# Pacing and pinning the modulation and gate steps of a two-layer hybrid decoder trunk

## The chip, the cores and the metric

The kernel runs on one core of one Trainium2 chip. The metric is the time of one execution on the device, in microseconds; the median of the runs is compared. The profile shows one execution, with the core's engines: PE (TensorE, matrix multiply; PEld is its weight load), DVE (VectorE), ACT (ScalarE), POOL (GpSimd) and SP (SyncE, which here issues every DMA).

## The reference, cut to what matters

Two decoder layers over 512 tokens of width 1024, all in float32. Each layer does this:

```python
shift, scale, gate = split(silu(c) @ w_ada + b_ada, 3)
h = rms_norm(x, ln_pre) * (1 + scale) + shift
u = split_columns(h @ w_in)
o_a = dilated_attention(u['a_q'], u['a_k'], u['a_v'])
o_b = nsa_attention(u['b_q'], ...)
o_c = rms_norm(gla_attention(u['c_q'], u['c_k'], u['c_v'], log_a), gla_norm)
o_d = banded_attention(u['d_q'], u['d_k'], u['d_v'], SWA_WIN - 1, sinks)
mixed = concat([o_a * silu(u['a_z']), ..., o_d * silu(u['d_z'])])
x = x + gate * rms_norm(mixed @ w_out, ln_post)
```

What the change moves about is the first line: the product of the one row `silu(c)` with the 1024 x 3072 matrix `w_ada` of a layer. It depends on no other work of the layer. Two thirds of it, shift and scale ("modulation"), are needed when the next layer begins; the last third ("gate") when the layer ends.

## The kernel before, in words

Matrices are multiplied in two parts: every weight tile `wraw` that comes from memory is split into a rounded part `whi` (ScalarE, L478) and the rest `wlo` (VectorE, L481), every activation into HH and HL, and three matmuls make one product. For each chunk of 128 columns of `w_in`, `mm_T` (L528) issues 24 matmuls of 512 columns; `mm_TM` (L540) is the same with tokens and columns exchanged; `fin_T` and `fin_tm` empty the accumulators on ScalarE and VectorE (for the compressed keys by the copies `x`, L619 and L621). `proj` (L652) goes through all chunks, `out1` (L1226) does the output projection as far as groups C, B and A reach, and `out2` (L1248) the rest with the norm and the residual add.

The four attention groups run in the order C, B, A, D. `attn_c` (L822) is a chain of products over levels of a chunked linear attention (the tiles zp, dp, bp, kq, att, oc); the others consist of `unit` (L755): scores on PE, maximum and mask on VectorE (L766), exponential on ScalarE (L768), scaling on VectorE (L777, L779), transposes on PE (L782), copies back (L787, L789).

**The first line of the reference runs on VectorE.** `extras` (L362) is a generator that goes through units of work, one per turn. For layer 0 these are 32 modulation steps for layer 1 (`mod`, L288: one multiply-and-sum of a 128 x 512 tile `wmod` with the broadcast row, L293) and then 16 gate steps (`mac`, L349: the tile `wada` times one value per partition, added to `aac`, L351 and L353). For layer 1 there are the 16 gate steps alone. The gate comes in two halves of 8 steps; when a half is done, `fin` (L373) adds over the partitions with a matmul of a matrix of ones (`ada`, L380), adds the bias (`adab`, VectorE, L381) and multiplies by the norm's weights (`gl`, POOL, L383). Each step's tile, 256 KB, is loaded one step ahead, by SP, into a pool of two buffers (`ad`), which the two rows that `fin` loads (L377, L379) share. `out2` reads `gl` at L1284.

**What orders the work.** The program is traced in one order; a scheduler then sets each engine's order ahead of the run: among the instructions that its own model of the machine takes as ready, the one traced first goes first. `pin()` (L524) adds an edge that keeps the PE instructions of a block behind PE's projection matmul traced last, without a wait on its result. On the chip every engine works through its own order, and so does SP's queue, where a load waits until its buffer is free.

`merge` (L1310) makes the order of the trace. It goes through the stages (attention C, B, A and four parts of D), takes a step of attention, then as many steps of the projection `pg` as a ratio of estimated costs allows; the generators yield these costs (1.3 for six matmuls of `mm_T`; 24 (n + 8) / 2400 for one `mm_TM`). Every projection cost goes through `bg`, which counts it up and takes one turn of `extras` for each `pace` that is full:

```python
            def bg(cost):
                tick[0] += cost
                while tick[0] > pace:
                    tick[0] -= pace
                    next(BG[0], None)
```

`pace` comes from the list TK of the layer, by stage (C, B, A, all of D). Whatever of `extras` is left behind the stages is traced at L1378. The first turn of `extras` only loads; each later turn does one unit.

Of the kernel before, what the change touches and what calls it, by code (L numbers as in the profile page):

```python
# [7 lines left out]
F32 = mybir.dt.float32  # L8
F32R = mybir.dt.float32r
AF = mybir.ActivationFunctionType  # L10
ALU = mybir.AluOpType
# [31 lines left out]
STP = 0  # L43

LP = [
    dict(HC=30, HB=[60, 60, 60, 200, 200, 200, 200, 120], HA=60, HD=200, RC=0.9, RB=0.7, RA=1.4, RD=0.8, TK=[1.5, 1.5, 1.5, 1.5], PT=(4, 3),
         HO=(0, 2, 1, 3)),
    dict(HC=30, HB=[60, 60, 60, 60, 60, 60, 60, 200], HA=100, HD=30, RC=0.9, RB=0.8, RA=0.8, RD=1.4, TK=[1.0, 6.0, 1.2, 0.7], PT=(1, 0),
         HO=(0, 3, 1, 2)),
]  # L50
WLO_MOD, WLO_POOL = 5, ()
# [182 lines left out]
def build(tc, A, out_d):  # L234
    nc = tc.nc
    PE, ACT, DVE, POOL, SP = nc.tensor, nc.scalar, nc.vector, nc.gpsimd, nc.sync
    with ExitStack() as ctx:
        def pool(name, bufs, **kw):
            return ctx.enter_context(tc.tile_pool(name=name, bufs=bufs, **kw))
# [8 lines left out]
        ad_p = pool('ad', B['ad'])  # L248
# [9 lines left out]
        def ps_t(tag, name):  # L258
            return ps.tile([128, 512], F32, tag=tag, name=name)
# [4 lines left out]
        def s_t(name, n, bufs=None):  # L264
            return sm_p.tile([128, n], F32, tag=name, name=name, **({'bufs': bufs} if bufs else {}))
# [16 lines left out]
        def load_mod(l, n, p, tag):  # L282

            wt = p.tile([128, 512], F32, tag=tag, name='wmod')
            SP.dma_start(out=wt, in_=A['w_mod'][l, n // 4, n // 2 % 2, n % 2])
            return wt

        def mod(l, n, wt, ss, gs):  # L288

            o, c = _P['bada'][0], n // 2  # L290
            h = n % 2
            init, dst = (tmp[:, c:c + 1], ss[:, c:c + 1]) if h else (pars[l][:, o + c:o + c + 1], tmp[:, c:c + 1])
            DVE.tensor_tensor_reduce(wt, wt, csr[:, 512 * h:512 * h + 512], 0.5, init, ALU.mult, ALU.add, dst)  # L293
            if n % 4 == 3:
                j = n // 4
                o = _P['lnpre'][0]
                DVE.scalar_tensor_tensor(gs[:, j:j + 1], ss[:, c:c + 1], 1.0, pars[l][:, o + j:o + j + 1], op0=ALU.add, op1=ALU.mult)
# [3 lines left out]
        def load_par(l):  # L301
            t = pp.tile([128, P_TOT], F32, tag='par', name='par')
            SP.dma_start(out=t, in_=A['par'][l])
            pars.append(t)

        WR = {}
        for ch in FIRST:
# [8 lines left out]
            elif ch in 'TQ':  # L316
                n = 'tm_c' if ch == 'T' else 't_cqk'
                WR[n] = [raw_p.tile([128, 1024 if ch == 'Q' else 996], F32, tag='raw', name='wraw')]
                SP.dma_start(out=WR[n][0], in_=A['w_in'][0, W_OFF[n, 0]:W_OFF[n, 0] + 128 * WR[n][0].shape[1]].rearrange('(p n) -> p n', p=128))
            else:  # L320
                i = len(x_t)
# [7 lines left out]
        ones = cp.tile([128, 1], F32, name='ones')  # L329
# [19 lines left out]
        def mac(acc, w, k, first):  # L349
            if first:  # L350
                DVE.tensor_scalar(acc, w, csil[:, k:k + 1], None, op0=ALU.mult)  # L351
            else:
                DVE.scalar_tensor_tensor(acc, w, csil[:, k:k + 1], acc, op0=ALU.mult, op1=ALU.add)  # L353

        def halves(t):
# [3 lines left out]
            DVE.tensor_tensor(out=lo, in0=t, in1=hi, op=ALU.subtract)  # L359
            return hi, lo  # L360

        def extras(l):  # L362

            units = []
            if l + 1 < DEPTH:
                load_par(l + 1)
                ss, gs = s_t('adass', 16, 2), s_t('adags', 8, 2)
                ada[l + 1] = (gs, ss)
                units = [(2, n) for n in range(32)]
            units += [(n, k) for n in range(2) for k in range(8)]  # L370
            gl[l] = []

            def fin(n, sb):  # L373
                acc = ps_t('s', 'ada')
                o = 512 * n
                br = ad_p.tile([128, 512], F32, tag='ad', name='adab')
                SP.dma_start(out=br, in_=A['rows'][l, 0, :, o:o + 512].to_broadcast([128, 512]))  # L377
                lr = ad_p.tile([128, 512], F32, tag='ad', name='adal')
                SP.dma_start(out=lr, in_=A['rows'][l, 1, :, o:o + 512].to_broadcast([128, 512]))  # L379
                PE.matmul(acc, ones.to_broadcast([128, 128]), sb, start=True, stop=True)  # L380
                DVE.tensor_tensor(out=br, in0=acc, in1=br, op=ALU.add)  # L381
                g = sz_p.tile([128, 512], F32, tag='sz', name='gl')
                POOL.tensor_tensor(out=g, in0=br, in1=lr, op=ALU.mult)  # L383
                gl[l].append(g)

            def load(n, k):
                if n == 2:
                    return load_mod(l + 1, k, ad_p, 'ad')
                wt = ad_p.tile([128, 512], F32, tag='ad', name='wada')
                SP.dma_start(out=wt, in_=A['w_gate'][l, n, k])  # L390
                return wt
            nxt = load(*units[0])
            prev = None
            for u, (n, k) in enumerate(units):
                yield
                wt = nxt
                if prev:
                    fin(*prev)
                    prev = None
                if n == 2:  # L400
                    mod(l + 1, k, wt, ss, gs)
                else:
                    if k == 0:
                        sb = ad_p.tile([128, 512], F32, tag='aac', name='aac', bufs=1)
                    mac(sb, wt, k, k == 0)
                    if k == 7:
                        prev = (n, sb)
                if u + 1 < len(units):
                    nxt = load(*units[u + 1])
            yield  # L410
            fin(*prev)

        gl, ada = {}, {}
# [61 lines left out]
        def split_w(raw, n, eng=None):  # L475
            hi = w_p.tile([128, n], F32R, tag='whi', name='whi')
            lo = w_p.tile([128, n], F32R, tag='wlo', name='wlo')
            ACT.copy(hi, raw)  # L478
            nsplit[0] += 1
            eng = eng or (POOL if nsplit[0] % WLO_MOD in WLO_POOL else DVE)  # L480
            eng.tensor_tensor(out=lo, in0=raw, in1=hi, op=ALU.subtract)  # L481
            return hi, lo

        def load_piece(l, name, i, kk, ncol):
# [39 lines left out]
        def pin():  # L524

            return tc.issue_after(LASTP[0]) if LASTP[0] is not None else nullcontext()
# [125 lines left out]
        def proj(l, skip=0):  # L652
            for n_, (name, cols) in enumerate(CHUNKS[skip:]):
                n = len(cols)
                w = WS[l].get(len(_parts(name, cols)))
                WS[l].ahead(PRE)
                yield 0.0
                if name.startswith('tm'):
                    for i in range(4):
                        fin_tm(l, name, i, mm_TM(l, w, i, n))  # L660
                        yield 24 * (n + 8) / 2.4e3
                elif name == 't_cqk':
                    for j in range(2):
                        fin_T(l, ('cq', 'ck')[j], (yield from mm_T(l, w, 128 * j, 128)))
                        yield 1.3
                else:
                    fin_T(l, name, (yield from mm_T(l, w, 0, n)))
                    yield 1.3
# [634 lines left out]
        def run(g):  # L1303
            for _ in g:
                pass
# [4 lines left out]
        def merge(l, pg, steps):  # L1310

            acc = 0.0
            tick = [0.0]
            done = False
# [5 lines that stand above are left out]
                    next(BG[0], None)  # L1320
            for n_, (g, names, ratio, lead) in enumerate(steps):
                pace = LP[l]['TK'][min(n_, 3)]
                while not all(n in T for n in names):
                    bg(next(pg))
                lead = list(lead)
                while True:
                    n = lead.pop(0) if len(lead) > 1 else lead[0]
                    tc.cur_priority -= n
                    cost = next(g, None)
                    tc.cur_priority += n  # L1330
                    if cost is None:
                        break
                    acc += cost * ratio
                    while acc > 0 and not done:
                        d = next(pg, None)
                        if d is None:
                            done = True
                        elif d < 0:
                            break
                        else:  # L1340
                            acc -= d
                            bg(d)
            if not done:
                run(pg)

        x1 = dr.tile([512, 1024], F32, tag='x1', name='x1', bufs=1)
        WS[0] = Stream(0, 2)
# [2 lines left out]
        def chain(*gs):  # L1350
            for g in gs:
                yield from g
# [8 lines left out]
        for l in range(DEPTH):  # L1361
# [4 lines left out]
            pg = chain(proj(l, 1 if l else 2), out1(l))  # L1366
# [51 lines left out]
```

## Time and profile before

| what | value |
|---|---|
| median of 3 runs | 699.97 us (698.76 to 700.46) |
| the profiled execution's own time | 701.64 us |
| its span, first to last instruction | 699.9 us |
| mean granted clock of TensorE | 0.979 |
| busy: PE, PEld, DVE, ACT, POOL | 648.1, 525.2, 496.6, 332.1, 30.0 us |
| chain that ended last, by engine | PE 62%, DVE 16%, DMA 7%, ACT 6%, issue 5%, SPq 2% |

The span is that of the one execution that the profile shows; some 1.7 us of its time lie outside. Matmuls are pipelined and their ends are modelled, so PE is marked busy even where it is not at its peak. PEclk is the clock that the throttle granted, as a share of 2.4 GHz; 0.5 is 1.2 GHz. "Idle before" is the time in which an engine stood still before an instruction, with what ended it.

The stages can be told by their instructions: attention C of layer 0 runs from some 57 to 147 us, B to 245, A to 300, D to 342 (with the output projection), `out2` and the head of the next layer to 386; attention C of layer 1 to 480, B to 575, A to 640, the rest to the end.

### The profile page before, as it was taken

What the parts mean: (1) busy time and instruction counts of PE and PEld (TensorE: products, weight loads), DVE (VectorE), ACT (ScalarE), POOL (GpSimd) and SP (SyncE); (2) the same over time, 40 slices, a digit from 0 to 9 for tenths busy, and PEclk for the clock granted to TensorE, in tenths of its full rate; (3) what the DMA queues carried; (4) which work ended last, traced back from release to release, by engine and by line L of the source; (5) the groups of instructions that cost most, each with busy time, mean ns of one, the idle gap of its engine ahead of it and who ended that gap; (6) DMA issues with size and microseconds to landing.
All of it is one profiled execution on the core that took longest, in us unless ns stands there. A gap on an engine that the chain in (4) does not pass through costs nothing.

```text
span 699.9 us, 11964 instructions
## 1 busy us (share of the span) xinstructions
PE 648.1 (93%) x4460; PEld 525.2 (75%) x4460; DVE 496.6 (71%) x1291; ACT 332.1 (47%) x744; POOL 30.0 (4%) x57
## 2 busy tenths in 40 slices
PE   3997888899999999999998978999999999999996
PEld 1775776787677777679986756888777877778895
DVE  5994878675978765785598458464398778757756
ACT  5454443172556554573476236246346346434532
POOL 2000001000000000000011000000000000000000
PEclk9999899899999999999999989999999999999999
DMA  8957755566342412002642772212620021011233
GB/s 296 391 224 199 225 183 168 159 200 236 101 131 79 162 45 75 33 16 76 210 164 84 233 191 75 62 62 66 206 61 23 10 90 46 31 45 46 76 124 118
DMA packets 38163, 87.89 MB, mean 126 GB/s; under 512 B 4185, under 2 KB 7769, under 8 KB 38106
## 3 DMA queue, kind: packets, MB, share of 16 engines
q1 hardware_dynamic: 38106, 87.14, 38.9%
q8 instruction: 35, 0.57, 0.3%
q14 instruction: 22, 0.18, 0.1%
HBM read 81.88 MB, written 5.24 MB: 124 GB/s over the span
## 4 chain that ended last, share of the span: by engine, by line
PE 62%; DVE 16%; DMA 7%; ACT 6%; issue 5%; SPq 2%; POOL 1%; DVEq 0%; POOLq 0%; ACTq 0%
PE mmT L534 22%; PE yo L1221 9%; PE mmTM L547 7%; PE pT L782 5%; DVE wmod L293 3%; DMA wmod<-in_w_mod 3%; PE ob L796 3%; PE sc L649 2%; DMA wada<-in_w_gate 2%; DVE wlo L481 2%; PE yo L1268 2%; PE sc L650 2%; PE oa L796 2%; PE od L1055 2%; ACT whi L478 1%
## 5 line engine op out<-in xcount | busy, mean ns | idle before, releaser
L534 PE MATMUL mmT<-HH,whi 128*128 128x512 f32 (+1 forms) x352 | 146.4, 416 | 6.8 <-ACT x L619 6.8
L534 PE MATMUL mmT<-HL,whi 128*128 128x512 f32 (+1 forms) x352 | 142.3, 405 | 0.0
L534 PE MATMUL mmT<-HH,wlo 128*128 128x512 f32 (+1 forms) x352 | 141.9, 404 | 0.0
L768 ACT ACTIVATE p<-p,m 128x256 f32<-128x256 f32 (+3 forms) x128 | 68.8, 539 | 79.6 <-DVE m L766 76.8
L481 DVE TENSOR_TENSOR wlo<-wraw,whi 128x1024 fp32r<-128x1024 f32 (+3 forms) x60 | 72.1, 1202 | 28.1 <-ACT whi L478 27.8
L478 ACT CAST whi<-wraw 128x1024 fp32r<-128x1024 f32 (+3 forms) x60 | 61.4, 1026 | 53.5 <-PE mmT L534 29.9
L534 PEld LDWEIGHTS mmT<-HH,whi 128*128 128x128 f32 (+1 forms) x352 | 67.4, 191 | 25.0 <-ACT x L619 8.3
L534 PEld LDWEIGHTS mmT<-HH,wlo 128*128 128x128 f32 (+1 forms) x352 | 67.0, 190 | 15.2 <-issue 1.2
L534 PEld LDWEIGHTS mmT<-HL,whi 128*128 128x128 f32 (+1 forms) x352 | 67.2, 191 | 13.1 <-issue 1.0
L766 DVE CUSTOM_DVE_ANT_0 p<-sc,cst 128x128 f32<-128x128 f32 (+3 forms) x96 | 44.8, 481 | 16.1 <-PE sc L650 15.6
L782 PE MATMUL pT<-cst,p 128*128 128x128 f32 x296 | 49.1, 279 | 4.7 <-DVE p L779 1.9
L547 PE MATMUL mmTM<-whi,HH 128*128 128x256 f32 (+1 forms) x160 | 48.6, 304 | 2.9 <-ACT HH L470 2.4
L782 PEld LDWEIGHTS pT<-cst,p 128*128 128x128 f32 x296 | 33.5, 140 | 20.0 <-issue 8.8
L547 PE MATMUL mmTM<-whi,HL 128*128 128x256 f32 (+1 forms) x160 | 48.0, 300 | 0.4 <-DVE HL L471 0.4
L547 PE MATMUL mmTM<-wlo,HH 128*128 128x256 f32 (+1 forms) x160 | 47.6, 298 | 0.0
L1221 PE MATMUL yo<-whi,HL 128*128 128x256 f32 x144 | 41.5, 289 | 0.0
L1221 PE MATMUL yo<-whi,HH 128*128 128x256 f32 x144 | 41.5, 288 | 0.0
L1221 PE MATMUL yo<-wlo,HH 128*128 128x256 f32 x144 | 41.5, 288 | 0.0
L789 DVE COPY pt<-pT 128x256 f32<-128x256 f32 (+3 forms) x60 | 28.9, 500 | 10.6 <-PE pT L782 7.8
L547 PEld LDWEIGHTS mmTM<-whi,HH 128*128 128x128 f32 x160 | 31.3, 196 | 5.7 <-ACT HH L470 3.5
L293 DVE CUSTOM_DVE_ANT_0 wmod<-wmod,csr,par 128x512 f32<-128x512 f32 x32 | 23.6, 746 | 13.7 <-DMA wmod<-in_w_mod 13.7
L649 PE MATMUL sc<-k,x 128*128 128x128 f32 (+3 forms) x96 | 32.1, 344 | 1.0 <-DVE m L766 1.0
(274 smaller groups left out, 1340.2 us busy)
## 6 DMA issues: line engine op xcount, KB each, us to landing
wraw<-in_w_in SPq DMA_DIRECT2D x52, 512.0 KB
wmod<-in_w_mod SPq DMA_DIRECT2D x64, 256.0 KB
wada<-in_w_gate SPq DMA_DIRECT2D x32, 256.0 KB
wor<-in_w_out SPq DMA_DIRECT2D x12, 512.0 KB
w<-in_w SPq DMA_DIRECT2D x8, 512.0 KB
vs<-vd SPq DMA_DIRECT2D x24, 128.0 KB
x<-in_x SPq DMA_DIRECT2D x8, 256.0 KB
wor<-in_w_out SPq DMA_DIRECT2D x8, 256.0 KB
```

What stands on the lines that cost most here:

```text
L293: DVE.tensor_tensor_reduce(wt, wt, csr[:, 512 * h:512 * h + 512], 0.5, init, ALU.mult, ALU.add, dst)
L478: ACT.copy(hi, raw)
L481: eng.tensor_tensor(out=lo, in0=raw, in1=hi, op=ALU.subtract)
L534: LASTP[0] = PE.matmul(acc[:m], a, b, start=(n == 0), stop=(n == 23)).ins
L547: LASTP[0] = PE.matmul(acc[:, :ncol], a, b, start=(n == 0), stop=(n == 23)).ins
L649: PE.matmul(out, q[e][:, qs], k[e][0][:, ks], start=True, stop=False)
L766: DVE.tensor_tensor_reduce(p[:, c], sc[:, c], mask, -0.125, 1e38 if sink is None else sink[0][:, es[j]:es[j] + 1], ALU.add, ALU.min, m[:, ...
L768: ACT.activation(p[:, c], p[:, c], AF.Exp, bias=m[:, j:j + 1], scale=-1.0, accum_out=lsum[:, j:j + 1])
L782: PE.transpose(tp[:, b:b + 128], p[:, b:b + 128], C('ident'))
L789: DVE.tensor_copy(dst, src)
L796: PE.matmul(o[hs, q0:q1], vt[:, kb, vc:vc + 64], PT[:, 512 * kb:512 * kb + q1 - q0], start=(first and kb == 0), stop=(last and kb == 3), s ...
L1221: LASTP[0] = PE.matmul(acc[:, :n_], a, b, start=(n == 0), stop=(n == last)).ins
```

## The change

The paces become other numbers, with a fifth for the projection steps that are left when the stages are through; at the start of each stage the count is cut to the stage's pace. `fin`'s matmul is pinned behind PE's projection matmul traced last, and `fin` comes four turns later than before. The VectorE instructions of each modulation and gate step get an edge that keeps them behind VectorE's instruction traced last at that moment (the object LO only tells which engine that is). The loads are not pinned. All arithmetic stays the same.

```diff
@@ -43,9 +43,9 @@
 STP = 0
 
 LP = [
-    dict(HC=30, HB=[60, 60, 60, 200, 200, 200, 200, 120], HA=60, HD=200, RC=0.9, RB=0.7, RA=1.4, RD=0.8, TK=[1.5, 1.5, 1.5, 1.5], PT=(4, 3),
+    dict(HC=30, HB=[60, 60, 60, 200, 200, 200, 200, 120], HA=60, HD=200, RC=0.9, RB=0.7, RA=1.4, RD=0.8, TK=[3.0, 2.0, 1.8, 1.0, 1.2], PT=(4, 3),
          HO=(0, 2, 1, 3)),
-    dict(HC=30, HB=[60, 60, 60, 60, 60, 60, 60, 200], HA=100, HD=30, RC=0.9, RB=0.8, RA=0.8, RD=1.4, TK=[1.0, 6.0, 1.2, 0.7], PT=(1, 0),
+    dict(HC=30, HB=[60, 60, 60, 60, 60, 60, 60, 200], HA=100, HD=30, RC=0.9, RB=0.8, RA=0.8, RD=1.4, TK=[99.0, 2.5, 2.0, 2.0, 2.0], PT=(1, 0),
          HO=(0, 3, 1, 2)),
 ]
 WLO_MOD, WLO_POOL = 5, ()
@@ -359,6 +359,11 @@
             DVE.tensor_tensor(out=lo, in0=t, in1=hi, op=ALU.subtract)
             return hi, lo
 
+        LO = [None]
+
+        def last_dve():
+            return next(i for i in reversed(nc.cur_bb.bb.instructions) if i.engine == LO[0].engine)
+
         def extras(l):
 
             units = []
@@ -377,7 +382,8 @@
                 SP.dma_start(out=br, in_=A['rows'][l, 0, :, o:o + 512].to_broadcast([128, 512]))
                 lr = ad_p.tile([128, 512], F32, tag='ad', name='adal')
                 SP.dma_start(out=lr, in_=A['rows'][l, 1, :, o:o + 512].to_broadcast([128, 512]))
-                PE.matmul(acc, ones.to_broadcast([128, 128]), sb, start=True, stop=True)
+                with pin():
+                    PE.matmul(acc, ones.to_broadcast([128, 128]), sb, start=True, stop=True)
                 DVE.tensor_tensor(out=br, in0=acc, in1=br, op=ALU.add)
                 g = sz_p.tile([128, 512], F32, tag='sz', name='gl')
                 POOL.tensor_tensor(out=g, in0=br, in1=lr, op=ALU.mult)
@@ -395,19 +401,24 @@
                 yield
                 wt = nxt
                 if prev:
+                    for _ in range(4):
+                        yield
                     fin(*prev)
                     prev = None
-                if n == 2:
-                    mod(l + 1, k, wt, ss, gs)
-                else:
-                    if k == 0:
-                        sb = ad_p.tile([128, 512], F32, tag='aac', name='aac', bufs=1)
-                    mac(sb, wt, k, k == 0)
-                    if k == 7:
-                        prev = (n, sb)
+
+                with tc.issue_after(last_dve()):
+                    if n == 2:
+                        mod(l + 1, k, wt, ss, gs)
+                    else:
+                        if k == 0:
+                            sb = ad_p.tile([128, 512], F32, tag='aac', name='aac', bufs=1)
+                        mac(sb, wt, k, k == 0)
+                if n < 2 and k == 7:
+                    prev = (n, sb)
                 if u + 1 < len(units):
                     nxt = load(*units[u + 1])
-            yield
+            for _ in range(4):
+                yield
             fin(*prev)
 
         gl, ada = {}, {}
@@ -478,7 +489,7 @@
             ACT.copy(hi, raw)
             nsplit[0] += 1
             eng = eng or (POOL if nsplit[0] % WLO_MOD in WLO_POOL else DVE)
-            eng.tensor_tensor(out=lo, in0=raw, in1=hi, op=ALU.subtract)
+            LO[0] = eng.tensor_tensor(out=lo, in0=raw, in1=hi, op=ALU.subtract).ins
             return hi, lo
 
         def load_piece(l, name, i, kk, ncol):
@@ -1320,6 +1331,7 @@
                     next(BG[0], None)
             for n_, (g, names, ratio, lead) in enumerate(steps):
                 pace = LP[l]['TK'][min(n_, 3)]
+                tick[0] = min(tick[0], pace)
                 while not all(n in T for n in names):
                     bg(next(pg))
                 lead = list(lead)
@@ -1340,8 +1352,10 @@
                         else:
                             acc -= d
                             bg(d)
+            pace = LP[l]['TK'][4]
             if not done:
-                run(pg)
+                for d in pg:
+                    bg(max(d, 0))
 
         x1 = dr.tile([512, 1024], F32, tag='x1', name='x1', bufs=1)
         WS[0] = Stream(0, 2)
```

## Rows read from the trace of the kernel before

**Rows 1.** The page, part 1: busy us, share of the span, instructions.

```profile
PE 648.1 (93%) x4460; PEld 525.2 (75%) x4460; DVE 496.6 (71%) x1291; ACT 332.1 (47%) x744; POOL 30.0 (4%) x57
```

**Rows 2.** Table by stage: us, busy of PE, PEld, DVE, ACT, POOL, clock, DMA, GB/s.

```profile
57.00:147.00 90.00, 75.73 (x718) 63.82 (x718) 67.34 (x159) 37.01 (x59) 2.95 (x6) 0.91 0.61 184
147.00:245.00 98.00, 95.23 (x583) 73.32 (x582) 75.86 (x208) 50.92 (x129) 3.79 (x4) 1.00 0.45 149
245.00:300.00 55.00, 54.23 (x274) 39.62 (x273) 37.44 (x120) 30.89 (x88) 1.22 (x2) 1.00 0.16 49
...
342.00:386.00 44.00, 39.84 (x272) 36.29 (x271) 37.09 (x77) 28.04 (x69) 7.31 (x14) 1.00 0.42 145
386.00:480.00 94.00, 87.19 (x780) 70.43 (x779) 53.66 (x99) 37.92 (x62) 3.95 (x5) 0.95 0.41 114
480.00:575.00 95.00, 93.30 (x580) 73.41 (x579) 69.67 (x203) 45.20 (x104) 1.50 (x4) 1.00 0.27 83
...
410.00:480.00 70.00, 66.74 (x696) 55.48 (x695) 42.38 (x83) 32.28 (x54) 3.95 (x5) 0.94 0.31 85
```

**Rows 3.** Waits of PE in c0, 57 to 147 us: us, times, longest.

```profile
PE att L926 <- DVE kq L916: 5.7, 2, 3.1
PE mmT L534 <- ACT x L619: 4.7, 2, 2.9
PE dp L866 <- DVE qkd L856: 3.1, 1, 3.1
```

**Rows 4.** Table of ten-microsecond windows inside c0, columns as in rows 2.

```profile
67.00:77.00 10.00, 7.75 (x28) 6.81 (x29) 7.46 (x16) 4.96 (x7) 0.00 (x0) 0.66 0.72 224
...
87.00:97.00 10.00, 7.06 (x47) 6.11 (x46) 9.72 (x23) 3.98 (x8) 0.00 (x0) 1.00 0.62 202
...
107.00:117.00 10.00, 7.39 (x88) 5.69 (x86) 9.52 (x23) 3.55 (x6) 1.46 (x2) 0.83 0.50 155
...
127.00:137.00 10.00, 6.93 (x90) 6.45 (x90) 6.75 (x22) 0.89 (x2) 0.00 (x0) 0.71 0.47 158
```

**Rows 5.** Instruction groups of DVE in c0: busy us, mean ns, idle before, releaser.

```profile
L293 DVE CUSTOM_DVE_ANT_0 wmod<-wmod,csr,tmp 128x512 f32<-128x512 f32 x16 | 12.0, 748 | 3.6 <-DMA wmod<-in_w_mod 3.4
L293 DVE CUSTOM_DVE_ANT_0 wmod<-wmod,csr,par 128x512 f32<-128x512 f32 x16 | 11.9, 747 | 13.7 <-DMA wmod<-in_w_mod 13.7
```

**Rows 6.** Chain that ended last, in order of time: start, us, what.

```profile
57.69 9.40 DMA wmod<-in_w_mod
...
117.10 5.17 DMA wmod<-in_w_mod
```

**Rows 7.** Instruction groups of DVE at the head of c1, 386 to 412 us.

```profile
L353 DVE SCALAR_TENSOR_TENSOR aac<-wada,csil,aac 128x512 f32<-128x512 f32 x7 | 5.3, 750 | 10.1 <-DMA wada<-in_w_gate 9.8
```

**Rows 8.** Timeline of PE at the head of c1: start, us, instruction, idle before.

```profile
408.24 2.07 PE L380 MATMUL ada<-aac,ones 128*128 128x512 f32 x2 [3.55 <-DVE aac L353]
...
413.95 0.62 PE L534 MATMUL mmT<-HH,whi 128*128 128x512 f32 x1
```

**Rows 9.** Tile wada on DVE, 140 to 245 us: duration ns min/median/max, first and last.

```profile
L353 DVE SCALAR_TENSOR_TENSOR aac<-wada,csil,aac x21: 732/747/752, 146.9 to 241.2; 128x512 f32<-128x512 f32 x21
L351 DVE TENSOR_SCALAR aac<-wada,csil x3: 468/478/486, 145.0 to 212.9; 128x512 f32<-128x512 f32 x3
```

**Rows 10.** Timeline of ACT at the head of c1.

```profile
405.52 1.04 ACT L478 CAST whi<-wraw 128x1024 fp32r<-128x1024 f32 x1 [7.67 <-DMA wraw<-in_w_in]
```

**Rows 11.** Timeline of SP's queue at the head of c1.

```profile
394.25 1.13 SPq L390 DMA_DIRECT2D wada<-in_w_gate  x2
395.43 1.16 SPq L490 DMA_DIRECT2D wraw<-in_w_in  x2
```

**Rows 12.** Instruction groups of DVE in out0, 342 to 386 us.

```profile
L353 DVE SCALAR_TENSOR_TENSOR aac<-wada,csil,aac 128x512 f32<-128x512 f32 x1 | 0.8, 751 | 0.1
L381 DVE TENSOR_TENSOR adab<-ada,adab 128x512 f32<-128x512 f32 x1 | 0.7, 680 | 0.0
...
L351 DVE TENSOR_SCALAR aac<-wada,csil 128x512 f32<-128x512 f32 x1 | 0.5, 474 | 0.0
```

**Rows 13.** Timeline of SP's queue in c0.

```profile
90.74 5.68 SPq L285 DMA_DIRECT2D wmod<-in_w_mod  x3
97.67 0.33 SPq L490 DMA_DIRECT2D wraw<-in_w_in  x1
```

**Rows 14.** Waits of ACT in c0, 57 to 147 us: us, times, longest.

```profile
ACT whi L478 <- DMA wraw<-in_w_in: 2.8, 2, 2.4
```

## The prediction

> **What bounds the kernel now.** The busy shares come first: TensorE (PE) is marked busy for 93% of the span and VectorE (DVE) for 71% [rows 1]. A kernel with a full PE could gain nothing from moving VectorE's work, so the next view is the table by stage, to see whether PE is full everywhere. I call the stages c, b, a, d (the four attention groups) and out, with the layer's number behind. It isn't full: in c0 (57 to 147 us) PE is busy 75.73 of 90 us, 14.3 idle, and its granted clock averages 0.91; in b0 and a0 it idles 2.8 and 0.8 us at full clock; in c1 (386 to 480) it idles 6.8 us at 0.95; in b1 1.7 [rows 2]. The loss is in c0 and at the head of c1.
>
> Then: who ends those gaps? In c0 the list of PE's waits is short: VectorE's kq and qkd, and the copies of x, which run on VectorE and ScalarE in turn [rows 3]. PE also pays afterwards: the ten-microsecond windows around 67, 107 and 127 have granted clocks of 0.66, 0.83 and 0.71, a mixture of 1.2 and 2.4 GHz [rows 4]. A window loses (1 - clock) of its length, so 3.4 + 1.7 + 2.9, less half of the third window's 3.07 us of idleness: some 6.5 us.
>
> Why is VectorE late? It runs in order, and in c0 it has the 32 modulation steps of the next layer (L293): 23.9 us of work, and before them 17.1 us of idleness, ended by the step's own load [rows 5]. The chain shows it: it stands still for 9.40 us and, later, for 5.17 us on a wmod load [rows 6]. Everything VectorE does for attention C is queued behind. At the head of c1 the gate steps (L353) do the same: 7 steps, 10.1 us of waiting [rows 7]; the gate sum's matmul (L380) then stands in PE's queue, PE idles 3.55 us before it, and matmuls are still 0.62 us long at 414 [rows 8].
>
> **The change, part by part.** No instruction is removed; each of the 48 + 16 steps and 4 sums moves. I added up the costs that the projection's generators yield (L537, L661, L663, L668) and let the pacing loop run on them. Projection costs per stage are 50.9, 40.5 and 29.9 in c0, b0, a0, and 61.3, 47.0, 15.6 in layer 1.
>
> Before, pace 1.5 makes 33 calls in c0 (all 32 modulation steps) and the gates follow in b0; VectorE also takes 8 gates of layer 1 ahead of time there, so b0 has 24 [rows 9]. After: c0 gets 16 calls, 15 modulation steps; b0 21 calls, 17 modulation and 4 gate steps; a0 16 calls, 12 gates and a sum; the last sum falls in d0. In layer 1, c1 gets none (pace 99); b1 14 gates and a sum; a1 2 and a sum. The pin holds VectorE's part of a step behind what was traced just before, so no step can run ahead into another layer. Each step's load moves with it on SP. The new tail pacing finds nothing left to issue.
>
> *c0.* 17 of 32 steps go. Bound: c1 from 410 on has no step of this stream at all, and idles 3.3 us in 70 [rows 2]; 3.5 of c0's 14.3 would so remain, and 10.8 + 6.5 = 17.3 us is what all 32 steps cost. By number 17/32 of it, 9.2. But the waits should shrink more than in proportion: one call per 1.5 of cost is one per 1.5 x 90/50.9 = 2.65 us, less than the 5.17 us that a load took [rows 6]; at pace 3.0 it is some 5 us. I take 12; ends 5 (the qkd gap and half its slow clock) and 17.
>
> *Head of c1.* The gap of 3.55 us, and (1 - 0.95) x 94 = 4.7 us of slow clock, together 8.2. What is late next: the weight cast (L478) waits until 405.5 for its load, 7.67 us [rows 10]; SP had issued that load at 395.4, behind two gate loads [rows 11], and with those gone it lands earlier. I take 5; ends 0 and 8.
>
> *out0 (342 to 386).* Two gate steps and a sum leave VectorE, 0.8 + 0.7 + 0.5 = 1.9 us [rows 12] of 37.1 busy in 44. I take 1; ends 0 and 2.
>
> *What b and a pay.* The trace prices a step there: b0, with 24 gates and two sums, lasts 98 us; b1, with none, 95 [rows 2, 9]. That is 0.13 us per step; the upper end is its whole 0.75 us [rows 5]. b0 has 3 steps fewer and no sum: 0.5 gained. a0 gets 12 and a sum: between 1.6 and 9.7, I take 2.5. b1, 14 and a sum: 1.9 to 11.2, I take 3. a1 and d0, 2 steps and 2 sums: 0.3 to 2.9, I take 0.5. The cover is VectorE's idle time in a0 and b1 (17.6 and 25.3 us); I stay near the low end because b0, the nearest row, is the same chain of scores, softmax and transposes.
>
> *The sum four steps later.* It takes away the one wait of PE that a sum causes (in the head above). Elsewhere it is free: 4 calls are 13 us in a0 (4 x 1.8 x 55/29.9) and 20 in b1, and the last step is done by then.
>
> *The queues.* SP is in order too: at 90.7 it needed 5.68 us for three wmod loads, each held until a buffer comes free [rows 13], and weight loads stand behind it. With the pin that holding can grow. ScalarE's casts waited 2.8 us in all of c0 for weight loads [rows 14], behind four raw buffers; I cost it at nothing, which ends if a hold exceeds the PE time of the buffered weights. POOL has the four products (L383); the copies kl and the rstd powers behind them aren't needed before the products' rows have long arrived, so nothing is counted there.
>
> **Sum.** 12 + 5 + 1 + 0.5 - 2.5 - 3 - 0.5 = 12.5 us gained. The profiled execution took 701.64 us (span 699.9, 1.7 around it), so 689.1; the median of the runs is 1.7 below that execution, so 687.5, say **688**.
>
> After the 3.1 us gap before dp (66 to 69 us) the clock fell to 0.66, while the 2.9 us wait for x (89 to 92 us) left its window, 87 to 97, at 1.00 [rows 3, 4]. The Trainium skill ("TensorE: Matmul & The Clock Gate", section HAM oscillation) says that waits between bursts of matmuls return the engine to its lower clock and are paid again in slow work. By that rule each microsecond of idleness in c0 counts for more than one; by the rows only some gaps do. Taken for every gap, it would lead to the far end of c0's 17.
>
> **The rivals.**
> *Larger gain.* Every listed stall goes and steps cost 0.13: 17 + 8 + 2 + 0.5 - 4 = 23.5 us, **676**. For it: c1 without steps idles little. Against: 15 steps remain in c0.
>
> *Slower.* In b and a the steps come between the softmax's instructions, and each delays the chain by its whole 0.75 us: 28 x 0.75 + 3 x 0.69 = 23 us against 18 gained, **705**. It decides from 18/28 = 0.64 us per step on. For it: the pin sets the step directly behind the softmax, where before it could fill a gap. Against: b0's row. If c0 also gains only its 5, it is 714.
>
> *No change.* The pinned order may put VectorE's steps where they still wait for their loads, and what c0 gains b1 and a0 give back: **700**. Each engine's work stays the same, which is for it; the idle time and slow clock of c0 are against. The Trainium skill ("Perfetto Trace Analysis", section Identifying Performance Opportunities) holds that generally one improves the most-contended engine; read strictly, a move that shortens none of TensorE's work would leave the time alone. The table by stage disagrees: TensorE is that engine, but not in c0.
>
> **How the numbers follow.** Forecast 0.59, larger gain 0.22, no change 0.06, slower 0.13. A measurement of this kernel tells some 0.3% (2 us) from no change. Faster: 0.81; same 0.06; slower 0.13. The range runs from 675, the larger gain's end, to 704, where two thirds of the slower cases are left out: a0 and b1 near their upper ends with c0 as taken.
>
> **What would show it.** Right: PE's idle time between 57 and about 135 falls to some 5 us with a clock of 0.96 or more; VectorE's waits for wmod loads fall from 17.1 to under 5; no gate step stands before b1, and c1 shows no gap before a sum; b1 and a0 grow by 3 us each at most. Wrong: b1 or a0 longer by 8 us or more; ScalarE's casts waiting for weight loads behind a held SP; PE's gaps in c0 still ended by kq, meaning that attention C's own chain was the limit and the steps only filled it.

## The result, and the profile after

The changed kernel took 690.45 us (median of 4 runs, 688.79 to 694.38), the kernel before 700.22 (698.76 to 701.06) beside it: ratio 0.9864, 95% interval 0.9832 to 0.9895. The profiled execution has a span of 689.2 us against 699.9, and a mean granted clock of 0.991 against 0.979. The forecast was 688 in a range of 675 to 704.

The engines' work is nearly what it was [rows 1]. Page of the changed kernel, part 1:

```profile
PE 642.8 (93%) x4460; PEld 520.9 (76%) x4460; DVE 496.7 (72%) x1291; ACT 332.3 (48%) x744; POOL 30.5 (4%) x57
```

Table by stage of the changed kernel (us, busy of PE, PEld, DVE, ACT, POOL, clock, DMA, GB/s), cut at round times as in [rows 2]:

```profile
57.00:137.00 80.00, 71.22 (x717) 59.50 (x716) 55.57 (x118) 36.34 (x59) 2.96 (x6) 0.96 0.48 145
137.00:235.00 98.00, 96.26 (x596) 75.32 (x595) 74.35 (x231) 52.02 (x133) 1.22 (x2) 1.00 0.38 125
...
372.00:465.00 93.00, 87.94 (x803) 73.12 (x804) 51.47 (x97) 42.49 (x70) 2.69 (x4) 0.98 0.33 96
465.00:560.00 95.00, 91.80 (x557) 72.11 (x555) 69.38 (x197) 43.36 (x100) 2.78 (x5) 1.00 0.32 107
```

Against [rows 2], c0 is shorter, with a clock of 0.96 for 0.91; the b stages are no shorter. Round times don't show where 10.7 us went, so both traces are cut again at the same TensorE instructions: the first zp matmul of attention C, the first matmul into ms (C is done), the last matmul of the output projection's main part. The same table of the kernel before, cut there (c0; b0 to d0; out0 and the head of c1; c1 from zp on; b1 to d1):

```profile
61.60:145.10 83.50, 69.99 (x694) 59.70 (x695) 63.42 (x150) 33.98 (x55) 2.69 (x4) 0.90 0.59 178
145.10:340.10 195.00, 191.40 (x1174) 150.40 (x1173) 139.01 (x398) 102.77 (x266) 5.28 (x8) 1.00 0.34 110
340.10:414.50 74.40, 66.69 (x375) 55.85 (x374) 51.14 (x96) 35.94 (x80) 7.31 (x14) 0.95 0.54 170
414.50:481.10 66.60, 63.34 (x690) 53.42 (x690) 40.96 (x81) 32.81 (x55) 3.95 (x5) 0.97 0.27 74
481.10:672.90 191.80, 188.77 (x1168) 150.79 (x1167) 138.70 (x418) 89.59 (x217) 2.71 (x6) 1.00 0.23 69
```

And of the changed kernel:

```profile
63.10:135.70 72.60, 64.92 (x689) 54.90 (x690) 50.90 (x110) 32.93 (x55) 2.69 (x4) 0.95 0.48 143
135.70:331.90 196.20, 191.75 (x1171) 150.82 (x1170) 145.42 (x431) 103.13 (x265) 5.80 (x8) 1.00 0.38 122
331.90:399.30 67.40, 61.85 (x372) 53.67 (x370) 43.79 (x86) 35.96 (x80) 6.03 (x13) 1.00 0.48 151
399.30:466.10 66.80, 63.50 (x691) 53.75 (x691) 41.03 (x81) 32.91 (x55) 2.69 (x4) 0.97 0.23 72
466.10:662.20 196.10, 191.62 (x1172) 151.67 (x1171) 151.84 (x436) 89.37 (x217) 5.29 (x8) 1.00 0.29 92
```

Row by row: c0 gives 10.9 us, b0 to d0 take 1.2, out0 and the head of c1 give 7.0, c1 takes 0.2, b1 to d1 take 4.3. The stretch before c0 takes 1.5, the end nothing. In sum 10.7, the difference of the spans. Of the 1.5 us before c0, some 1.4 are no loss: six matmuls of the projection, 0.23 us apart, that stood behind the first zp matmul now stand ahead of it. TensorE's records up to that matmul, before and after (the last row holds one of zp itself):

```profile
0.00:61.60 61.60, 47.46 (x220) 35.87 (x221) 46.73 (x121) 28.90 (x53) 5.89 (x16) 1.00 0.84 294
0.00:63.10 63.10, 48.81 (x227) 36.98 (x227) 47.09 (x120) 29.84 (x54) 5.78 (x16) 1.00 0.80 286
```

Four of the six come out of c0 (693 matmuls, now 689), so c0's 10.9 us contain 0.9 of this shift; up to the first ms matmul the gain is 9.4 us (145.1 to 135.7).

In c0 the second column splits the gain: TensorE's idle time falls from 13.5 to 7.7 us (83.50 - 69.99; 72.60 - 64.92), its busy time by 5.1, with the clock up from 0.90 to 0.95. Some 0.9 of the 5.1 are the four matmuls that moved. So with each microsecond of idleness went some 0.7 of slow work. The Trainium skill ("TensorE: Matmul & The Clock Gate", section HAM oscillation) has it that idle gaps are paid again in slow work; summed over the stage, these rows agree. Who waits is seen in the waits between 57 and 137 us, VectorE's for the steps' loads, PE's three longest, and ScalarE's for weight loads (us, times, longest):

```profile
DVE wmod L293 <- DMA wmod<-in_w_mod: 5.3, 2, 2.9
```

```profile
PE att L937 <- DVE kq L927: 3.0, 2, 1.8
PE dp L902 <- DVE u L892: 1.9, 1, 1.9
PE mmT L545 <- ACT x L630: 1.3, 1, 1.3
```

```profile
ACT whi L489 <- DMA wraw<-in_w_in: 4.4, 2, 4.2
```

The load waits went from 17.1 [rows 5] to 5.3 us, PE's three longest waits from 13.5 [rows 3] to 6.2. At the head of c1 the chain of waits has no wada load and no ada sum any more:

```profile
374.32 3.62 PE mmTM L558 x22
377.94 21.42 PE mmT L545 x94
399.36 1.08 PE zp L858 x8
```

The projection runs through in 21.4 us; before, a sum with 3.55 us of idleness stood in it [rows 8]. ScalarE's weight casts there no longer wait for a load [rows 10]: the longest wait, 3.93 us at 394, is for PE. In the whole row (out0 and the head of c1) TensorE's idle time falls by 2.2 us (7.71 to 5.55) and its busy time by 4.8; of that, the two sums, which now stand in b1 to d1, had 3.1: 1.02 at 372 us and, at a lower clock, 2.07 at 408 [rows 8].

### The profile page after: what moved, and what is told of

The parts are those of the page before. It is cut to its first block, busy times and chain, and to the rows that moved or that the text cites. A ratio compares the mean times of both kernels' runs of the same rounds, so it can differ in the third digit from the quotient of the medians.

```text
span 689.2 us, 11949 instructions
## 1 busy us (share of the span) xinstructions
PE 642.8 (93%) x4460; PEld 520.9 (76%) x4460; DVE 496.7 (72%) x1291; ACT 332.3 (48%) x744; POOL 30.5 (4%) x57
## 4 chain that ended last, share of the span: by engine, by line
PE 61%; DVE 15%; DMA 9%; ACT 8%; issue 4%; POOL 1%; SPq 0%; DVEq 0%; POOLq 0%; ACTq 0%
PE mmT L545 23%; PE yo L1232 9%; PE mmTM L558 6%; PE pT L793 4%; DMA wmod<-in_w_mod 3%; PE ob L807 3%; DMA wraw<-in_w_in 3%; DVE wlo L492 2%; ACT whi L489 2%; PE yo L1279 2%; PE od L1066 2%; DVE wmod L293 2%; DVE p L777 2%; PE sc L660 2%; PE oa L807 2%
## 5 line engine op out<-in xcount | busy, mean ns | idle before, releaser
L545 PE MATMUL mmT<-HH,whi 128*128 128x512 f32 (+1 forms) x352 | 142.5, 406 | 3.9 <-ACT x L630 3.4
L545 PE MATMUL mmT<-HH,wlo 128*128 128x512 f32 (+1 forms) x352 | 139.8, 398 | 0.0
L545 PEld LDWEIGHTS mmT<-HH,whi 128*128 128x128 f32 (+1 forms) x352 | 65.8, 187 | 19.4 <-ACT x L630 4.7
L558 PEld LDWEIGHTS mmTM<-wlo,HH 128*128 128x128 f32 x160 | 31.0, 194 | 1.0 <-issue 0.8
```

The lines of the kernel that those rows point to most:

```text
L545: LASTP[0] = PE.matmul(acc[:m], a, b, start=(n == 0), stop=(n == 23)).ins
L558: LASTP[0] = PE.matmul(acc[:, :ncol], a, b, start=(n == 0), stop=(n == 23)).ins
```

## The experiments

Each expectation names its own theories by letters. Two main questions: which part of the change brings the gain, and what makes b1 to d1 longer by 4.3 us. "c0", "the head" (out0 with it) and so on are cut as above.

**The parts alone.** First the paces without the rest: the kernel before with the new TK, the cut of the count and the paced tail; no pins, sums not later. In the cuts of the code below, only the entry TK is shown of a long line.

```diff
-TK=[1.5, 1.5, 1.5, 1.5]
+TK=[3.0, 2.0, 1.8, 1.0, 1.2]
-TK=[1.0, 6.0, 1.2, 0.7]
+TK=[99.0, 2.5, 2.0, 2.0, 2.0]
+                tick[0] = min(tick[0], pace)
...
```

> The changed kernel's paces without its pins and without the later sums. If the paces carry the gain (theory A: fewer steps in c0, none in c1), it comes within 3 us of the changed kernel, 690 to 693, with about 15 modulation steps in c0. If the pins carry it (theory B: without them steps run ahead and VectorE stands before their loads), it stays near 698 to 701, because steps traced later are still taken ahead of time as soon as a buffer is free; then more than 20 modulation steps stand in c0, and gates of layer 1 stand ahead of b1.

694.86 us, ratio 0.9918 (0.9894 to 0.9943): some 60% of the gain, between the times of the two theories. c0 takes 74.5 us, the head 67.9, b0 to d0 198.7, b1 to d1 192.5. The signs that theory B named are there: 22 modulation steps stand in c0, and eight of layer 1's gate steps run ahead into a0 and d0 of layer 0. VectorE's steps in c0:

```profile
L293 DVE CUSTOM_DVE_ANT_0 wmod<-wmod,csr,tmp x11: 747/752/1100, 68.3 to 134.9; 128x512 f32<-128x512 f32 x11
L293 DVE CUSTOM_DVE_ANT_0 wmod<-wmod,csr,par x11: 741/750/752, 69.0 to 136.3; 128x512 f32<-128x512 f32 x11
```

Then the rest without the paces: the changed kernel with the old ones.

```diff
-TK=[3.0, 2.0, 1.8, 1.0, 1.2]
+TK=[1.5, 1.5, 1.5, 1.5, 1.5]
-TK=[99.0, 2.5, 2.0, 2.0, 2.0]
+TK=[1.0, 6.0, 1.2, 0.7, 0.7]
```

> The pins and the later sums with the old paces. Theory A: c0 keeps its 32 modulation steps and its gaps, the head of c1 its gates, so 698 to 703. Theory B: 690 to 693, with VectorE's waits for wmod loads in c0 under 6 us although 32 steps stand there.

713.56 us, ratio 1.0202 (1.0171 to 1.0232): a miss for both theories: the pins alone (with the later sums) are slower. Chain of waits of this kernel, 379 to 421 us:

```profile
398.67 7.30 DMA wada<-in_w_gate
...
406.85 3.00 DMA wada<-in_w_gate
...
410.72 5.57 DMA wada<-in_w_gate
...
419.54 1.12 PE ada L386 x2
```

With a pin no gate step can run ahead into b0, where eight of layer 1's stood before [rows 9]. Under the old pace of 1.0 all sixteen now stand from the head of c1 on: eight and a sum at the head, paying three waits for loads, the other eight and the second sum between 424 and 447 us, inside c1. The head takes 80.1 us for 74.4, and c1 72.0 for 66.6, at a clock of 0.88. In these runs the pins pay only with paces that put no step there.

**The paces undone one layer at a time.** The changed kernel with the first of these two lines, then with the second.

> The changed kernel with the old paces in layer 0 only. Theory A: the 10.9 us that c0 won are lost again and the 2 us that a0 and d0 paid come back: 690.5 + 9 = 699. Theory B: 690 to 692.

698.95 us, ratio 0.9991 (0.9974 to 1.0008), where theory A had it: c0 is 81.6 us, b0 to d0 are 198.6, and the gain is gone.

> The changed kernel with the old paces in layer 1 only. Theory A: the head of c1 loses its 7 us again and b1 and a1 give their 4 us back: 693 to 694, with gates standing at the head of c1. Theory B: 690 to 692.

702.49 us, ratio 1.0042 (1.002 to 1.0063): further than either theory had it, for the reason just seen: 80.7 in the head and 70.6 in c1, 17 us above the changed kernel instead of the 7 that eight steps and both sums had cost. b1 to d1 are 191.9, as before the change.

**What a step costs in c0.** No modulation step in c0 at all:

```diff
-TK=[3.0, 2.0, 1.8, 1.0, 1.2]
+TK=[99.0, 1.2, 1.2, 1.0, 1.2]
```

> Paces 99, 1.2, 1.2, 1.0 in layer 0: no step in c0, all 48 from b0 on, one per 2.9 us there. If VectorE's steps are what still lengthens c0 (72.6 us against 66.7 in c1, which has more projection work and no steps), c0 falls to 57 to 62. Theory A: b0's compressed branch pays some 6 us for the steps in its chain, the rest is free, 682 to 687. Rival D (the waits for loads decide, and 2.9 us are less than the 5.0 that a load takes to land): b0 and a0 pay more than 10 us, 690 to 697.

688.16 us, ratio 0.9825 (0.9797 to 0.9853), the fastest kernel of the study with its whole output, though its interval overlaps that of the changed kernel. Table by stage, c0 and b0 to d0:

```profile
61.90:128.60 66.70, 63.46 (x690) 53.62 (x690) 40.97 (x82) 32.81 (x55) 2.69 (x4) 0.97 0.31 96
128.60:330.10 201.50, 192.97 (x1172) 150.98 (x1171) 157.05 (x462) 104.10 (x265) 7.22 (x8) 1.00 0.43 135
```

c0 is now as long as c1, 66.7 us and not the 57 to 62 expected: 30 steps between zp and ms cost the kernel before 16.8 us. The 14 steps that the changed kernel had kept there cost 5.9. But these and one that stood just before zp cost 5.3 us again in b0 to d0, 0.35 per step; the time lies between the two theories.

To part the loads from the products, the kernel with layer 0's old paces, in which the modulation steps read the resident csr instead of a loaded tile:

```diff
-            SP.dma_start(out=wt, in_=A['w_mod'][l, n // 4, n // 2 % 2, n % 2])
+            if l == 0:
+                SP.dma_start(out=wt, in_=A['w_mod'][l, n // 4, n // 2 % 2, n % 2])
...
-            DVE.tensor_tensor_reduce(wt, wt, csr[:, 512 * h:512 * h + 512], ...
+            DVE.tensor_tensor_reduce(wt, wt if l == 0 else csr[:, 512 - 512 * h:1024 - 512 * h], csr[:, 512 * h:512 * h + 512], ...
```

> Old paces in layer 0 with the pins (as in the run with old paces in layer 0, 698.95 us, c0 81.6 us from zp to ms), but the 32 modulation steps read a row that is in place instead of a loaded tile: the modulation of layer 1 has other values, VectorE's work stays, the loads and their waits go. If c0 is long because VectorE waits for loads in its order: c0 under 72, time 688 to 690. If it is long by VectorE's 24 us of work alone: c0 78 or more, 695 to 699.

694.93 us, ratio 0.9923 (0.9898 to 0.9948), between the two theories. c0 of the kernel with loads, then of this one:

```profile
61.20:142.80 81.60, 68.61 (x694) 57.69 (x694) 58.49 (x135) 33.40 (x55) 2.44 (x4) 0.92 0.52 159
```

```profile
63.00:139.20 76.20, 66.39 (x687) 55.78 (x688) 57.14 (x134) 32.36 (x54) 2.45 (x4) 0.93 0.26 79
```

Both have 24 steps there, the first of them begun just before zp. Of their 14.9 us over the 66.7 of a c0 without steps, the loads make 5.4 and the products with VectorE's place 9.5, 0.40 per step. This is one profile each, and one order gave lengths of c0 up to 3 us apart (see the end), so the split is rough; the medians, 698.95 and 694.93, are 4.0 apart.

**What b1 to d1 pay.** First guess: the steps in b1 stand in its opening. The count starts only after seven steps of attention B:

```diff
-                pace = LP[l]['TK'][min(n_, 3)]
+                hold, nst = n_ == 1 and l in (1,), 0
+                pace = 99.0 if hold else LP[l]['TK'][min(n_, 3)]
...
+                    nst += 1
+                    if hold and nst == 7:
+                        pace, tick[0] = LP[l]['TK'][1], 0.0
```

> The changed kernel, but in b1 the gate steps begin only when attention B's compressed branch is traced (its seventh step); the pace from there on is the same. From the first ms matmul to the first matmul of the compressed branch's result (ob from pct) b1 took 37.4 us before and 42.5 after the change. Theory A (a step costs where it stands in a chain of VectorE's instructions, and nothing elsewhere): that stretch goes back to 37 to 38 and nothing is paid later, 685 to 686. Rival B (each step costs about the same, some 0.3 us, wherever it stands): the 5 us appear later, 689 to 691.

690.52 us, ratio 0.9865 (0.9836 to 0.9893): the opening is short again (37.8 us to the first ob matmul, 42.5 in the changed kernel), but b1 to d1 take 197.0. Next guess: VectorE's products. Layer 1 leaves out twelve of the sixteen, and keeps loads and sums:

```diff
-                        mac(sb, wt, k, k == 0)
+                        if l == 0 or k in (0, 7):
+                            mac(sb, wt, k, k == 0)
```

> The changed kernel without VectorE's part of 12 of layer 1's 16 gate steps (k = 1 to 6 of either half); their loads stay, so the gate of layer 1 sums two of eight products per half. Theory A: the stretch from ms to the compressed result goes back to 37 to 38 us, 685 to 686, as in the kernel with late steps. Rival B: 12 steps at 0.3 us, 686 to 687, of which under 2 us in that stretch. Rival C (the steps cost by their loads in SP's queue): no change, 690 to 691.

690.82 us, ratio 0.987 (0.9841 to 0.9898), b1 to d1 197.5: twelve products of 0.75 us less, the opening short again (37.7 us), and nothing gained. So it isn't VectorE's work; rival C, the loads, has the time right and is answered by the last kernel of this group. The pins, then: none in layer 1, for steps or sums.

```diff
-                with pin():
+                with (pin() if l == 0 else nullcontext()):
...
-                with tc.issue_after(last_dve()):
+                with (tc.issue_after(last_dve()) if l == 0 else nullcontext()):
```

> The changed kernel, but in layer 1 the gate steps and their sums are not pinned; paces and the four steps' delay stay, layer 0 keeps its pins. Theory A (the 4.3 us that layer 1's b to d stages grew by are the pins': they hold TensorE's and ScalarE's order in b1 and a1 to another one, in which the projections stand elsewhere among the attention): b1 to d1 go from 196.1 back to about 192.5, the time is 686 to 687.5. Theory B (the steps cost there wherever they stand in these stages, by their loads and sums): 196 stays, 690 to 691.

691.1 us, ratio 0.9887 (0.9865 to 0.991), b1 to d1 196.1. Not the pins, and not the number of steps: without pins, eight of the sixteen run ahead into layer 0, as they did with the paces alone, and with half of the steps the stages are as long. And not the stage, when all sixteen go to a1 and d1:

```diff
-TK=[99.0, 2.5, 2.0, 2.0, 2.0]
+TK=[99.0, 99.0, 1.2, 1.0, 1.0]
```

> The changed kernel with paces of 99, 99, 1.2, 1.0, 1.0 in layer 1: all sixteen gate steps stand pinned in a1 and d1, none in b1. Theory A (pins that stand inside the attention cost, in whichever stage): b1 is 37.4 to its end of the head, the rest 159 to 161 instead of 153.6, time 690 to 692. Theory B (it is b1's order alone that cost): b1 to d1 about 192, time 686.

689.95 us, ratio 0.9871 (0.9846 to 0.9895), b1 to d1 196.4, at the lower end of theory A's range, though its reason, the pins, has just fallen. What all of these share, and the kernels with some 192 us (before, the pins alone, and layer 1's old paces) lack, is the two gate sums on TensorE inside b1 to d1. PE's timeline of the changed kernel at the first of them, and VectorE's:

```profile
541.62 1.02 PE L386 MATMUL ada<-aac,ones 128*128 128x512 f32 x2
...
545.20 0.50 PE L660 MATMUL sc<-k,x 128*128 128x512 f32 x1 [0.70 <-DVE adab L387]
```

```profile
544.46 0.69 DVE L387 TENSOR_TENSOR adab<-ada,adab 128x512 f32<-128x512 f32 x1 [0.86 <-DMA adab<-in_rows]
```

A sum takes TensorE some 1.0 us in a stretch that has no gap. It also holds one of the two PSUM buffers that the scores use (tag s) until VectorE has added the bias row, which here had to wait for the row's load; the next score matmul stands for 0.70 us. The unpinned layer 1 has no such wait and is as long, so the buffer is not needed for it. So the sums' matmuls of layer 1 were left out:

```diff
-                acc = ps_t('s', 'ada')
+                acc = ps_t('s', 'ada') if l == 0 else None
...
-                with pin():
-                    PE.matmul(acc, ones.to_broadcast([128, 128]), sb, start=True, stop=True)
-                DVE.tensor_tensor(out=br, in0=acc, in1=br, op=ALU.add)
+                if l == 0:
+                    with pin():
+                        PE.matmul(acc, ones.to_broadcast([128, 128]), sb, start=True, stop=True)
+                DVE.tensor_tensor(out=br, in0=acc if l == 0 else sb, in1=br, op=ALU.add)
```

> The changed kernel without TensorE's matmuls of layer 1's two gate sums (VectorE's add reads the partial products instead of their sum over the partitions); steps, loads, pins and paces stay. Theory A (the sums themselves are part of the 4.3 us by which layer 1's b to d stages grew: their four TensorE records are 2.0 us busy there, and stood at the head of c1 before): b1 to d1 take 193.5 to 194.5 instead of 196.1, the span is 687 to 687.5 and the median 688 to 689. Theory B (the 4.3 us are waits and order alone, the sums run in gaps): 196, 690 to 691.

686.34 us, ratio 0.9804 (0.9778 to 0.9829). b1 to d1:

```profile
467.30:659.40 192.10, 189.02 (x1168) 151.03 (x1167) 150.21 (x436) 89.05 (x217) 5.82 (x8) 1.00 0.30 94
```

Against the changed kernel's 196.1, four of the 4.3 us are gone, twice what theory A expected; TensorE is 2.6 us less busy (its four ada records are 2.0) and 1.4 less idle. All sixteen steps stay with their loads, which answers rival C, and cost 0.3 us together (192.1 against 191.8). The paces alone are the kernel that doesn't fit: it has both sums in b1 to d1, with four ada records of the same 2.0 us, and needs only 192.5.

```profile
471.50:664.00 192.50, 189.82 (x1172) 151.37 (x1171) 145.35 (x428) 89.68 (x217) 5.27 (x8) 1.00 0.27 83
```

Its other matmuls are 1.0 us less busy in this row than before (189.82 - 2.0 against 188.77) and its idle time is 2.7 us. Like the unpinned layer 1 it has eight steps and both sums here; in layer 1 the two differ in the code only by the sums' four turns, and yet take 192.5 and 196.1. The steps and sums, wherever they stand, also change the order of the remaining instructions, and that order can win or lose a few microseconds. Leaving out the sums changed it too: 115 of TensorE's 1166 other matmuls in these stages stand elsewhere. So it is shown that the sums' records take 2.0 us and that these stages are shorter in the kernel without them; with both in place another order needs only 0.7 us more than before. How much of the four is the sums' own time and how much is order is not shown.

**An attempt at a better version.** Layer 1 without pins, and fewer steps in c0:

```diff
-TK=[3.0, 2.0, 1.8, 1.0, 1.2]
+TK=[5.0, 1.6, 1.5, 1.0, 1.2]
```

> As the kernel with layer 1 unpinned, and the modulation steps paced 5.0, 1.6, 1.5, 1.0, 1.2 in layer 0, so that fewer of them stand in c0. Theory A (steps in c0 cost more than in b0 and a0, and layer 1's pins cost 4): c0 about 69 instead of 72.6, b0 to d0 about 161 instead of 158 after the head, layer 1 as without pins: 684 to 686. Theory B (what c0 wins comes back one for one in b0 and a0, layer 1 stays): 690.

696.84 us, ratio 0.9973 (0.9955 to 0.9992): a miss. c0 is 70.1 us with 8 steps, as hoped, but b0 to d0 take 204.4. Ten-microsecond windows in d0 show where:

```profile
290.00:300.00 10.00, 9.96 (x73) 8.38 (x71) 9.15 (x37) 7.74 (x26) 1.30 (x1) 1.00 0.27 86
300.00:310.00 10.00, 7.13 (x47) 4.51 (x45) 8.65 (x33) 4.06 (x14) 0.00 (x0) 0.91 0.16 55
310.00:320.00 10.00, 9.63 (x59) 8.13 (x60) 4.85 (x14) 2.94 (x10) 0.00 (x0) 0.75 0.27 80
```

TensorE idles 2.9 us, and the clock is then 0.75, a mixture of 1.2 and 2.4 GHz; the changed kernel has no such gap. The longest single gap there, 1.83 us at 308.8, waits for VectorE's p, and no gate step stands on VectorE between 298 and 309.6 us; what in the order made it was not followed up. The kernel without steps in c0 stays the best.

Not tried: the sums at their old place with the steps still pinned.

## Why the prediction was right, point by point

- **What bounds, and the direction: right.** The loss was in c0 and at the head of c1, and VectorE's steps with their loads made it. With TensorE busy 93% before and after, the rival of no change (by the rule on the most-contended engine in the Trainium skill, "Perfetto Trace Analysis", section Identifying Performance Opportunities) fell: the engine was full on the whole, but not in those two stages.
- **c0, 12 us: 10.9 in this execution, 0.9 of it the shift of matmuls.** The count of 15 steps left came out (one stands just before zp). Its marks: the clock reached the 0.96 asked for and the load waits 5.3 us (under 5 was asked), but TensorE still idles 8.8 us between 57 and 137, not 5. The estimate that all 32 steps cost 17.3 us was close: 16.8 for the 30 between zp and ms. Taking more than in proportion was right too, by less than expected: the 14 left cost 5.9. The reason given, loads that come too fast, is only about a third of a step's price; the rest is VectorE's own work in the order (5.4 and 9.5 us for 24 steps). Of the signs of being wrong, kq still ends 3.0 us of PE's gaps, but that "attention C's own chain was the limit" is refuted: without steps c0 takes 66.7 us.
- **The head of c1 and out0, 5 and 1 us: 7.0.** Of its ends, 0 and 8 for the head, the upper was near. The mechanism is as predicted: the gap before the sum, the slow clock of this stretch (0.95, now 1.00) and the late weight load all went. Two sizes were missed: of the 4.7 us of slow clock, which were read from all of c1, 1.9 stay (0.98 over 93 us), and the sums' own 3.1 us of TensorE, which left this stretch, were no term of the sum.
- **What b and a pay, 0.13 us per step: the size fitted, in part by luck.** Layer 0's b to d took 1.2 us for 2.3 predicted, but 23 steps in another order took 197.6 and 198.6 (the pins alone, layer 0's old paces) where 24 had taken 195.0: the number of steps alone doesn't set it. Layer 1's took 4.3 for 3.3, but sixteen steps cost 0.3 of it in the kernel without sums, and 4.0 went with the sums. The step that failed is "The sum four steps later ... Elsewhere it is free": it looked at who waits for the sum's input and counted VectorE's 0.69 us, not TensorE's own 1.0 us in a stage that TensorE fills. How much beyond these 2.0 us the order made is open. A part of it is a move: the two sums had stood in out0 and the head, whose 7.0 us contain them.
- **The slower rival** (each step delays the softmax by its whole 0.75 us) is refuted for layer 1: twelve products less gave nothing. In b0 to d0 steps cost 0.35 us in one comparison, half of that price. The 714 given for it with c0 at 5 is 712 by its own terms (700 - 11 + 23).
- **The queues, at nothing:** right as far as seen; at the head no weight cast waits for a load. From 57 to 137 us the casts' waits for weight loads grew from 2.8 [rows 14] to 4.4 us. One of 4.2 us, at 57.9, stands just before zp, where TensorE's gap is 1.1 us against 0.8, so it cost little.
- **Not predicted:** that the pins alone are slower by 2%. The text knew that steps had run ahead into b0, but didn't ask what it was worth under the old paces (13.6 us, 713.56 against 699.92 in the same runs).

## What to carry to other kernels

Before moving side work by pace, ask for each place what the fullest engine does there: an instruction of that engine can cost its whole time in a stage without gaps, however well its inputs are prepared, while work of a half-idle engine may cost nearly nothing. A pin takes away the scheduler's freedom to run ahead, so it must be tried together with the paces that it needs; alone it may lose more than both gain. And where an edit reshuffles an order, cut the traces at the same instructions in every variant, and distrust a difference that one reshuffle alone shows.

## What was not expected of the hardware

The same instructions need not take the same time. The changed kernel and six experiments issue identical orders on every engine through c0, and c0 took 72.6, 69.9, 71.8, 71.6, 69.6, 71.4 and 71.1 us in their profiles. TensorE's busy time there was 63.1 to 64.9 us, at granted clocks of 0.98 to 0.95. Against the one profile of the kernel before, c0's gain is so 11 to 14 us, and up to the first ms matmul 9 to 12 (133.1 to 135.7 after 145.1): the term of 12 is met at the upper end. A stage's difference of under 3 us from one profile each isn't settled. In b1 to d1 the spread is smaller: with one order in four kernels (the changed one, layer 0's old paces with and without loads, no steps in c0) it took 196.1, 195.1, 194.7 and 195.7; with the old one in three (before, the pins alone, layer 1's old paces) 191.8, 191.8 and 191.9. So the 4.3 us there are 2.8 to 4.3.
